# A two-layer decoder trunk on one core: joins that go behind the weight splits they held up, a table made later, an output in halves, and wo's row pairs in another order

## The chip, the cores and the metric

The kernel runs on one core of a Trainium2 chip. The metric is the device time of one execution in microseconds (us); less is better. The engines are named as in the profile: PE (TensorE, matmuls), DVE (VectorE), ACT (ScalarE), POOL (GpSimd) and SP (SyncE, which issues most DMAs here).

## The reference

A residual stream x of 256 tokens by 2048 columns passes through two layers. Layer 0 is retention with 8 heads and then an MLP; layer 1 is multi-head latent attention (MLA) with shared keys and values, and then an MLP. All is float32.

```python
for layer in range(DEPTH):
    if layer < N_A_LAYERS:
        x = x + retention(rms_norm(x, norm_mix[layer]), ret_w_in[layer], ret_w_out[layer], ...)
    else:
        # k_nope, k_pe, v from rms_norm(x, kv_norm_in) @ mla_w_kv_down, normed, @ mla_w_kv_up
        x = x + mla_attention(rms_norm(x, norm_mix[layer]), mla_w_dq[j], ..., mla_w_o[j], k_nope, k_pe, v, ...)
    x = x + jnp.square(jax.nn.relu(rms_norm(x, norm_mlp[layer]) @ mlp_w1[layer])) @ mlp_w2[layer]
```

Retention ends in `o * rsqrt(mean(o * o) + eps)`, times `silu(gate)`, times the output weights. Rotary tables (cos and sin of position times frequency) are made for retention and, with 64 columns, for MLA.

## The kernel before, in words

**Products.** Every weight is read once from memory as float32 into a `raw` buffer (three of them), by a DMA on SP's queue. ACT casts it to a high half `wh` (L206), DVE subtracts that from the weight for the low half `wl` (L207); this subtraction is called a low part here. Activations are split in the same way, and each product is three matmuls: high by high (L392), high by low (L393), low by high (L394). Five `wh` and five `wl` buffers go round.

**Row pairs.** Most products go through `gemm_pair`, which calls `quad` (L311) once for each of eight chunks of 256 weight rows (a row pair) by 1024 columns. A plain row pair is eight products of two-by-two blocks, 24 matmuls, and two low parts of 1024 columns. A seven is done by a scheme with seven products, 21 matmuls, for which DVE also forms sums of the weight blocks (L346, L355, L356) and then makes four low parts, one of 512 columns and three of 1024. Sevens have four extra accumulators, p1, p5, p6 and p7, which must be joined to the result after the last seven. `kinds` says which row pairs are sevens and `order` in which order they come. Row pair names in the rows have the number last: d_315 is row pair 5 of the second half of the last group of `w2`.

**The joins.** At the end of each MLP the second half of `w2` ends with plain row pairs behind the last seven, so `sums_into_x` (L159) joins the extra accumulators to x early: ACT copies p1 and p5, DVE forms v and u (L166, L167) and then adds or subtracts them in six instructions on x[.][2] and x[.][3] (L169, L171); p5 goes to both x[.][3]. When the last row pair is done, `rest_into_x` (layer 0) or `outside` (layer 1) adds the remaining accumulators (L517, L1167). In layer 0 the row pairs come in the order 0, 2, 4, 6, 1, 3, 5, 7 with sevens 1 and 3, in layer 1 in the order 0, 2, 1, 4, 3, 5, 6, 7 with sevens 1, 3 and 5. Behind layer 0 comes MLA's product with the kv-down weights (kd, by `piece`, L269 to L271), behind that dqp; behind layer 1 only the output.

**The order of the work.** The program is written out in Python, piece by piece (a piece is a chunk of weights). `later(n, fn)` puts a function in a list, to be called n pieces on; `tick` advances the clock and calls what is due. Each engine has its own queue of instructions, which it works off in order; a scheduler decides the order within each, and `queued_behind(ins, before)` makes one instruction stand behind another on the same engine. `low_part[0]` is always the low part made last. When an instruction at the head of a queue waits, all behind it wait as well.

**The tables.** `sincos` (L539) computes a table's angles on POOL by some 25 instructions. That for MLA, named `tm_`, is queued 12 pieces after the start of the first product; `mla_tables` (L589) makes sixteen small DVE instructions from it (`petab`, L598 and L601), 20 pieces after. For every head and each half of the tokens POOL also computes o_m and o_r, the inverse root of retention's norm, in `rstd` (L184, L186), from a sum that ACT makes (L201); DVE then makes y from it (L737), and PE transposes y into `ytp` (L225).

**wo.** MLA's output weights go through `gemm_blocks` (L460): two blocks of columns by `piece`, and then a pair of blocks, `wop`, by `gemm_pair`, in which row pairs 3, 5, 6 and 7 (`FOUR`) are sevens.

Of the kernel before, what the change touches and what calls it, by code (L numbers as in the profile page):

```python
# [16 lines left out]
ALU = mybir.AluOpType  # L17
# [18 lines left out]
P = 128  # L36
NT = 2
S = NT * P
# [9 lines left out]
QUERY, FOUR = (3, 4, 6, 7), (3, 5, 6, 7)  # L48
# [4 lines left out]
C_INVR, C_INVM, C_MASK, C_ID, C_ALL = 0, 128, 160, 544, 672  # L53
# [13 lines left out]
def yoco(ctx: ExitStack, tc: tile.TileContext, a):  # L67
    nc = tc.nc
# [25 lines left out]
    queue, low_part, first_low = [], [None], [None]  # L94
    clock, count, ahead = [0], itertools.count(), [None, None]

    def later(n, fn):
        queue.append((clock[0] + n, next(count), fn))
# [56 lines left out]
    def into_x(done, c, p, step=2):  # L155
        for j in range(2):
            later(step * j, lambda j=j: done(2 * p + j, [c[t][j] for t in range(NT)]))

    def sums_into_x(c, name):  # L159

        o = {}
        for key in ("p1", "p5"):
            o[key] = f2k([512], f"{name}_{key}")
            nc.scalar.copy(o[key], c[key])
        v, u = (f2k([512], f"{name}_{i}") for i in "vu")
        nc.vector.tensor_tensor(v, c["p6"], o["p1"], op=ALU.add)  # L166
        nc.vector.tensor_tensor(u, c["p7"], v, op=ALU.add)  # L167
        for t, j, part in ((0, 2, o["p1"]), (1, 2, u), (0, 3, o["p5"]), (1, 3, o["p5"])):
            nc.vector.tensor_tensor(x[t][j], x[t][j], part, op=ALU.add)  # L169
        for t, part in ((0, v), (1, u)):  # L170
            nc.vector.tensor_tensor(x[t][3], x[t][3], part, op=ALU.subtract)  # L171

    def rest_into_x(done, c):
        for j, keys in ((2, ("c11", "c21")), (3, ("c12", "c22"))):
            done(j, [c[key] for key in keys])

    def gain(col):
        return gains[:, col : col + 1]
# [126 lines left out]
    def queued_behind(ins, before):  # L305
        tc.add_manual_dep(
            ins.ins, before.ins.name,
            mybir.DependencyInfo(mybir.DependencyClass.NoSync, mybir.DependencyReason.DATA), reason="order",
        )
# [59 lines left out]
    def gemm_pair(w, chunk0, act, kinds, name, done, order=None, inner=None):  # L369

        made = {}
        total, count = {}, {}
        for seven in kinds:
            for key in ("c11", "c12", "c21"):
                total[key] = total.get(key, 0) + (1 if seven else 2)
            for key in ("p1", "p5", "p6", "p7") if seven else ("c22", "c22"):
                total[key] = total.get(key, 0) + 1

        def get(key):
            if key not in made:  # L380
                if key in ("p6", "p7"):
                    both = two_banks(f"{name}_p67")
                    made["p6"], made["p7"] = both[:, 0], both[:, 1]
                else:
                    made[key] = bank("tp" if key[0] == "p" else "acc", [512], f"{name}_{key}")
            return made[key]

        def mm(key, lhs, rhs):
            dst, n = get(key), count.get(key, 0)
            count[key] = n + 1  # L390
            (ah, al), (bh, bl) = lhs, rhs
            nc.tensor.matmul(dst, ah, bh, start=n == 0, stop=False)  # L392
            nc.tensor.matmul(dst, ah, bl, start=False, stop=False)  # L393
            nc.tensor.matmul(dst, al, bh, start=False, stop=n == total[key] - 1)  # L394

        order = order or range(len(kinds))
        sevens = [n for n, i in enumerate(order) if kinds[i]]
        for n, i in enumerate(order):
            need(act, i + 1)
            while kinds[i] and act[i][1] is None:  # L400
                run_first()
            v, more = act[i]
            quad(w, chunk0 + i, (v, more if kinds[i] else None), mm, f"{name}{i}")
            if inner is not None and n == sevens[-1]:
                queue.append((clock[0] + 1, -1, lambda: inner(made, name)))
            if n == len(kinds) - 1:
                queue.append((clock[0] + 1, -1, lambda: done(made) if inner else pair_out(made, name, done)))
            tick()
# [51 lines left out]
    def gemm_blocks(w, chunk_of, w_pair, act, nk, name, done):  # L460

        n = nk // 4
        parts = Firsts(act)
        first = [accs(512, f"{name}{b}") for b in range(2)]
        for g in range(n - 1):
            for b in range(2):
                need(act, 2 * g + 2)
                piece(w, chunk_of(b) + g, first[b], parts, g, nk, 512, f"{name}{b}")
        for b in range(2):
            need(act, 2 * n)  # L470
            last_piece(w, chunk_of(b), first[b], parts, nk, 512, f"{name}{b}", lambda acc, b=b: done(b, acc))
        gemm_pair(w_pair, 0, act, [k in FOUR for k in range(8)], f"{name}p", lambda c: into_x(done, c, 1))

    def x_block_t(blocks, b, g0s, outs, name, sums):

# [38 lines left out]
    def add_to_x(acc, b, ss, name):  # L514
        for t in range(NT):
            for part in acc[t] if isinstance(acc[t], tuple) else (acc[t],):
                nc.vector.tensor_tensor(x[t][b], part, x[t][b], op=ALU.add)  # L517
            if ss is not None:
                square_sum(x[t][b], ss[1][t][:, b : b + 1], f"{name}_{t}{b}")

# [18 lines left out]
    def sincos(inv, w, name):  # L539

        n = NT * w

        def f2k(shape, name):
            return shaped(act_tile(name, F32).rearrange("p j i s -> p (j i s)"), shape)

        ang = f2k([NT, w], f"{name}_ang")
        for t in range(NT):
            nc.gpsimd.tensor_scalar(ang[:, t], inv, pos_f[:, t : t + 1], None, op0=ALU.mult)
        flat = ang.rearrange("p t w -> p (t w)")
        k = f2k([2, n], f"{name}_k")  # L550
        for i in range(2):
            nc.gpsimd.tensor_scalar(k[:, i], flat, 1 / (2 * PI), 0.25 * i, op0=ALU.mult, op1=ALU.add)
        nc.gpsimd.tensor_scalar(k, k, MAGIC, -MAGIC, op0=ALU.add, op1=ALU.add)
        kh = f2k([2, n], f"{name}_kh")
        nc.gpsimd.tensor_scalar(kh, k, MAGIC_HI, -MAGIC_HI, op0=ALU.add, op1=ALU.add)
        kl = f2k([2, n], f"{name}_kl")
        nc.gpsimd.tensor_tensor(kl, k, kh, op=ALU.subtract)
        r = f2k([2, n], f"{name}_rr")
        both = flat.unsqueeze(1).to_broadcast([P, 2, n])
        part = f2k([2, n], f"{name}_part")  # L560

        def less(dst, src, kk, c):
            nc.gpsimd.tensor_scalar(part, kk, c, None, op0=ALU.mult)
            nc.gpsimd.tensor_tensor(dst, src, part, op=ALU.subtract)

        less(r, both, kh, c1)
        for kk, c in ((kl, c1), (kh, c2), (kl, c2), (k, c3)):
            less(r, r, kk, c)
        nc.gpsimd.tensor_scalar(r[:, 1], r[:, 1], PI / 2, None, op0=ALU.add)
        nc.gpsimd.tensor_scalar(k, r, 1 / (2 * PI), MAGIC, op0=ALU.mult, op1=ALU.add)  # L570
        nc.gpsimd.tensor_scalar(k, k, -MAGIC, None, op0=ALU.add)
        for c in (c1, c2 + c3):
# [84 lines left out]
    def start(half):  # L657
        first_inputs(half)
        if half == 3:
            nc.sync.dma_start(pos_i, a["pos"])  # L660
            nc.sync.dma_start(cst, a["cst"])
            nc.sync.dma_start(gpe, a["gpe"])
        if half == 5:
            ret_tables()
        if half == 7:
            for b in range(NB):
                later(2 + b, lambda b=b: load_x(b))
            later(6, scale_tables)
            later(12, lambda: mla_sc.append(sincos(cst[:, C_INVM : C_INVM + 32], 32, "tm")))
            later(20, mla_tables)  # L670

    def ret_rope(acc, out, name, wait):

# [483 lines left out]
    def leave(t, b):  # L1157
        nc.sync.dma_start(a["out"][t * P : (t + 1) * P, b * 512 : (b + 1) * 512], x[t][b])
# [4 lines left out]
            leave(t, b)  # L1163

    def outside(c):
        for t, j, key in ((0, 2, "c11"), (1, 2, "c21"), (0, 3, "c12"), (1, 3, "c22")):
            nc.vector.tensor_tensor(x[t][j], c[key], x[t][j], op=ALU.add)  # L1167
            leave(t, j)

    mlp(1, act, r, finish)  # L1170
    while queue:
# [94 lines left out]
```

## Time and profile before

| what | value |
|---|---|
| median of 3 runs | 2466.27 us (2465.57 to 2467.79) |
| profiled execution, its own time | 2468.5 us |
| its span in the trace | 2466.7 us |
| mean granted clock of PE | 0.998 |
| DMA, mean over the span | 211 GB/s |
| last PE matmul starts | 2461.30 us |

In timelines a row has the start, the length in us, the engine, the line and operation, output and inputs, and how many equal instructions in a run it stands for; in brackets the idle time of the engine before it and what ended that. Instructions overlap a little with their successors, so the distance between two starts, not the length, is what one costs in a full queue. In the table of waits a row has the total, the number of times and the longest.

### The profile page before, as it was taken

The numbers are of one execution on the slowest core, as the hardware profiler recorded it, in microseconds if no ns is written. First come the engines' busy times: TensorE is split into PE (matmuls) and PEld (weight loads), VectorE is DVE, ScalarE is ACT, GpSimd is POOL, SyncE is SP. The second block draws the span as 40 slices with busy tenths as digits, with TensorE's granted clock in tenths as the row PEclk, the third lists the DMA queues.
The fourth block names the chain that finished last, engine by engine and source line by source line (L and its number), as shares of the span: only waits on it lengthen the run. The fifth ranks groups of instructions, "written<-read, shape, count | busy, mean of one in ns | idle before, by whom it ended". The sixth has DMA issues, their size and how long they took to land.

```text
span 2466.7 us, 31692 instructions
## 1 busy us (share of the span) xinstructions
PE 2447.1 (99%) x11605; PEld 2060.3 (84%) x11605; DVE 2210.9 (90%) x2917; ACT 1641.3 (67%) x2306; POOL 237.7 (10%) x287
## 2 busy tenths in 40 slices
PE   9999999999999999999999999999999999999998
PEld 7888888888888888888888788998888888888887
DVE  7799899889899999999999998777899999999998
ACT  6566666556677767667676677577677667676674
POOL 6300001000000010010110001101000100100100
PEclk9999999999999999999999999999999999999999
DMA  8555569556565596695786555444555876957864
GB/s 310 197 196 201 177 200 265 198 174 223 204 212 199 193 264 208 209 268 188 239 257 216 184 205 179 154 163 171 187 207 204 252 226 197 264 200 221 263 219 154
DMA packets 93404, 521.05 MB, mean 211 GB/s; under 512 B 11072, under 2 KB 12224, under 8 KB 40000
## 3 DMA queue, kind: packets, MB, share of 16 engines
q1 hardware_dynamic: 71856, 472.83, 55.7%
q0 software_dynamic: 21248, 46.15, 8.8%
q8 instruction: 91, 1.49, 0.2%
q14 instruction: 65, 0.53, 0.1%
q10 hardware_dynamic: 144, 0.05, 0.0%
HBM read 479.14 MB, written 39.85 MB: 210 GB/s over the span
## 4 chain that ended last, share of the span: by engine, by line
PE 97%; DVE 2%; ACT 0%; issue 0%; POOL 0%; DMA 0%; SPq 0%; ACTq 0%; DVEq 0%
PE u_c L394 7%; PE u_c L392 7%; PE u_c L393 7%; PE d_c L393 7%; PE d_c L394 7%; PE d_c L392 7%; PE rp_c L394 3%; PE rp_c L393 3%; PE rp_c L392 3%; PE rq_acc L297 2%; PE rk_acc L297 2%; PE u_p L394 2%; PE u_p L393 2%; PE u_p L392 2%; PE d_p L393 2%; PE d_p L394 2%
## 5 line engine op out<-in xcount | busy, mean ns | idle before, releaser
L207 DVE TENSOR_TENSOR u_wl<-u_raw,u_wh 128x1024 fp32r<-128x1024 f32 (+1 forms) x256 | 278.7, 1109 | 30.9 <-ACT u_wh L206 30.9
L207 DVE TENSOR_TENSOR d_wl<-d_raw,d_wh 128x1024 fp32r<-128x1024 f32 (+1 forms) x256 | 277.8, 1107 | 29.0 <-ACT d_wh L206 28.9
L393 PE MATMUL d_c<-d_wl,hid 128*128 128x512 f32 x706 | 275.8, 391 | 4.8 <-DVE d_wl L207 4.8
L392 PE MATMUL u_c<-u_wh,n 128*128 128x512 f32 x712 | 277.4, 391 | 0.0
L394 PE MATMUL u_c<-u_wh,n 128*128 128x512 f32 x712 | 277.2, 389 | 0.0
L393 PE MATMUL u_c<-u_wl,n 128*128 128x512 f32 x712 | 277.2, 389 | 0.0
L394 PE MATMUL d_c<-d_wh,hid 128*128 128x512 f32 x706 | 275.8, 391 | 0.0
L392 PE MATMUL d_c<-d_wh,hid 128*128 128x512 f32 x706 | 274.6, 392 | 0.5 <-ACT d_wh L206 0.5
L206 ACT CAST u_wh<-u_raw 128x1024 fp32r<-128x1024 f32 (+1 forms) x256 | 241.1, 973 | 48.0 <-PE u_c L394 21.2
L206 ACT CAST d_wh<-d_raw 128x1024 fp32r<-128x1024 f32 (+1 forms) x256 | 240.2, 972 | 42.8 <-ACT d_wh L206 16.0
L206 ACT CAST d_wh<-d_u 128x1024 fp32r<-128x1024 f32 x106 | 107.7, 1051 | 118.5 <-DVE d_u L356 65.4
L206 ACT CAST u_wh<-u_u 128x1024 fp32r<-128x1024 f32 x104 | 106.3, 1052 | 115.8 <-DVE u_u L356 59.5
L393 PEld LDWEIGHTS d_c<-d_wl,hid 128*128 128x128 f32 x706 | 133.0, 188 | 33.2 <-DVE d_wl L207 6.1
L394 PEld LDWEIGHTS u_c<-u_wh,n 128*128 128x128 f32 x712 | 133.7, 188 | 27.8
L206 ACT CAST rp_wh<-rp_raw 128x1024 fp32r<-128x1024 f32 x112 | 104.0, 945 | 79.3 <-PE rp_c L394 53.7
L392 PEld LDWEIGHTS d_c<-d_wh,hid 128*128 128x128 f32 x706 | 132.9, 188 | 28.4 <-ACT d_wh L206 1.4
L393 PEld LDWEIGHTS u_c<-u_wl,n 128*128 128x128 f32 x712 | 133.7, 188 | 27.3
L392 PEld LDWEIGHTS u_c<-u_wh,n 128*128 128x128 f32 x712 | 133.7, 188 | 27.1
L394 PEld LDWEIGHTS d_c<-d_wh,hid 128*128 128x128 f32 x706 | 133.0, 188 | 27.7
L207 DVE TENSOR_TENSOR rp_wl<-rp_raw,rp_wh 128x1024 fp32r<-128x1024 f32 x112 | 119.3, 1085 | 18.0 <-ACT rp_wh L206 17.9
L207 DVE TENSOR_TENSOR d_wl<-d_u,d_wh 128x1024 fp32r<-128x1024 f32 x106 | 125.5, 1217 | 0.0
L207 DVE TENSOR_TENSOR u_wl<-u_u,u_wh 128x1024 fp32r<-128x1024 f32 x104 | 123.1, 1217 | 2.0 <-ACT u_wh L206 1.6
(568 smaller groups left out, 6501.3 us busy)
## 6 DMA issues: line engine op xcount, KB each, us to landing
u_raw<-in_mlp_w SPq DMA_DIRECT2D x128, 1024.0 KB, 5.5
d_raw<-in_mlp_w SPq DMA_DIRECT2D x128, 1024.0 KB, 4.9
rp_raw<-in_ret_w_gv SPq DMA_DIRECT2D x56, 1024.0 KB, 4.9
ro_raw<-in_ret_w_out SPq DMA_DIRECT2D x32, 1024.0 KB, 5.0
uq_raw<-in_mla_w_uq SPq DMA_DIRECT2D x24, 768.0 KB, 4.3
rq_raw<-in_ret_w_qk SPq DMA_DIRECT2D x16, 1024.0 KB, 4.9
rk_raw<-in_ret_w_qk SPq DMA_DIRECT2D x16, 1024.0 KB, 4.9
xh<-d_c POOLq DMA_DIRECT2D x48, 256.0 KB, 6.1
```

The costliest lines, as they stand in the source:

```text
L206: nc.scalar.copy(h, src)
L207: return nc.vector.tensor_tensor(l, src, h.bitcast(F32), op=ALU.subtract)
L297: nc.tensor.matmul(acc[f], wh[:, cols], a.rearrange("p i s -> p (i s)"), start=k == 0, stop=k == nk - 1)
L392: nc.tensor.matmul(dst, ah, bh, start=n == 0, stop=False)
L393: nc.tensor.matmul(dst, ah, bl, start=False, stop=False)
L394: nc.tensor.matmul(dst, al, bh, start=False, stop=n == total[key] - 1)
```

## The change

1. `sums_into_x` is called two pieces instead of one after the last seven; its v and its additions are queued behind the low part made last by then, and the four instructions on x[.][3] come a piece later still (`join_rest`). In `rest_into_x` the additions for the second block of columns come half a piece after those for the first, and in `add_to_x` those of x[.][2] and x[.][3] at the end of layer 0 (`n2`) are queued behind the low part made last.
2. MLA's table is made 18 instead of 12 pieces after the start, and `mla_tables` comes at 26 instead of 20.
3. In `outside` the last block x[1][3] is added and written in two halves of 256 columns, one DMA on ACT's queue and one on SP's.
4. The pair of blocks of wo takes its row pairs in the order 0, 1, 2, 3, 5, 4, 6, 7.

```diff
-        nc.vector.tensor_tensor(v, c["p6"], o["p1"], op=ALU.add)
+        queued_behind(nc.vector.tensor_tensor(v, c["p6"], o["p1"], op=ALU.add), low_part[0])
         nc.vector.tensor_tensor(u, c["p7"], v, op=ALU.add)
-        for t, j, part in ((0, 2, o["p1"]), (1, 2, u), (0, 3, o["p5"]), (1, 3, o["p5"])):
-            nc.vector.tensor_tensor(x[t][j], x[t][j], part, op=ALU.add)
-        for t, part in ((0, v), (1, u)):
-            nc.vector.tensor_tensor(x[t][3], x[t][3], part, op=ALU.subtract)
+
+        def join(*parts):
+            for t, j, part, op in parts:
+                queued_behind(nc.vector.tensor_tensor(x[t][j], x[t][j], part, op=op), low_part[0])
+
+        join((0, 2, o["p1"], ALU.add), (1, 2, u, ALU.add))
+        join_rest = (0, 3, o["p5"], ALU.add), (1, 3, o["p5"], ALU.add), (0, 3, v, ALU.subtract), (1, 3, u, ALU.subtract)
+        queue.append((clock[0] + 1, -1, lambda: join(*join_rest)))
 
     def rest_into_x(done, c):
         for j, keys in ((2, ("c11", "c21")), (3, ("c12", "c22"))):
-            done(j, [c[key] for key in keys])
+            later(j / 2 - 0.5, lambda j=j, keys=keys: done(j, [c[key] for key in keys]))
...
-                queue.append((clock[0] + 1, -1, lambda: inner(made, name)))
+                queue.append((clock[0] + 2, -1, lambda: inner(made, name)))
...
+            lambda c: into_x(done, c, 1), order=(0, 1, 2, 3, 5, 4, 6, 7),
...
-                nc.vector.tensor_tensor(x[t][b], part, x[t][b], op=ALU.add)
+                added = nc.vector.tensor_tensor(x[t][b], part, x[t][b], op=ALU.add)
+                if name == "n2" and b >= 2:
+                    queued_behind(added, low_part[0])
...
-            later(12, lambda: mla_sc.append(sincos(cst[:, C_INVM : C_INVM + 32], 32, "tm")))
-            later(20, mla_tables)
+            later(18, lambda: mla_sc.append(sincos(cst[:, C_INVM : C_INVM + 32], 32, "tm")))
+            later(26, mla_tables)
...
-        for t, j, key in ((0, 2, "c11"), (1, 2, "c21"), (0, 3, "c12"), (1, 3, "c22")):
+        for t, j, key in ((0, 2, "c11"), (1, 2, "c21"), (0, 3, "c12")):
             nc.vector.tensor_tensor(x[t][j], c[key], x[t][j], op=ALU.add)
             leave(t, j)
+        for i, queue_ in enumerate((nc.scalar, nc.sync)):
+            part = slice(i * S, (i + 1) * S)
+            nc.vector.tensor_tensor(x[1][3][:, part], c["c22"][:, part], x[1][3][:, part], op=ALU.add)
+            queue_.dma_start(a["out"][P:, 3 * 512 + i * S : 3 * 512 + (i + 1) * S], x[1][3][:, part])
```

POOL's queue around the first head's o_m and o_r (so_931 and so_940 are the sums of the two token halves; `tm_` is MLA's table), before:

```order
L184 TENSOR_SCALAR o_m<-so_931 128x1
L186 TENSOR_TENSOR o_r<-o_m,neg_half 128x1
L548 TENSOR_SCALAR tm_ang<-cst,pos_f 128x32 x2
L552 TENSOR_SCALAR tm_k<-tm_ang 128x64 x2
L553 TENSOR_SCALAR tm_k<-tm_k 128x128
L555 TENSOR_SCALAR tm_kh<-tm_k 128x128
L557 TENSOR_TENSOR tm_kl<-tm_k,tm_kh 128x128
L563 TENSOR_SCALAR tm_part<-tm_kh 128x128
L564 TENSOR_TENSOR tm_rr<-tm_ang,tm_part 128x128
L184 TENSOR_SCALAR o_m<-so_940 128x1
L186 TENSOR_TENSOR o_r<-o_m,neg_half 128x1
```

and now (the lines lie four, later nine, further down in the changed file):

```order
L188 TENSOR_SCALAR o_m<-so_931 128x1
L190 TENSOR_TENSOR o_r<-o_m,neg_half 128x1
L188 TENSOR_SCALAR o_m<-so_940 128x1
L190 TENSOR_TENSOR o_r<-o_m,neg_half 128x1
L557 TENSOR_SCALAR tm_ang<-cst,pos_f 128x32 x2
```

The ten table instructions that stood between the two halves' pairs now stand behind both. On DVE the sixteen `petab` instructions stand together, ahead of the low parts of head 2's later weights, instead of in groups among those of head 1's.

DVE's queue at the end of layer 0's MLP, before (d_313 and d_315 are row pairs 3 and 5, d_317 the last; d_31_p the extra accumulators and their copies, x_mlp_12009 and x_mlp_12090 blocks of x):

```order
L207 TENSOR_TENSOR d_313_wl_12499<-d_313_u_12466,d_313_wh_12498 128x1024
L169 TENSOR_TENSOR x_mlp_12009<-x_mlp_12009,d_31_p_12508 128x512
L207 TENSOR_TENSOR d_315_wl_12525<-d_315_raw,d_315_wh_12524 128x1024
L166 TENSOR_TENSOR d_31_v<-d_31_p_12442,d_31_p_12508 128x512
L169 TENSOR_TENSOR x_mlp_12090<-x_mlp_12090,d_31_p_12510 128x512
L167 TENSOR_TENSOR d_31_u<-d_31_p_12442,d_31_v 128x512
L169 TENSOR_TENSOR x_mlp_12090<-x_mlp_12090,d_31_p_12510 128x512
L169 TENSOR_TENSOR x_mlp_12009<-x_mlp_12009,d_31_u 128x512
L171 TENSOR_TENSOR x_mlp_12090<-x_mlp_12090,d_31_v 128x512
L171 TENSOR_TENSOR x_mlp_12090<-x_mlp_12090,d_31_u 128x512
L207 TENSOR_TENSOR d_315_wl_12541<-d_315_raw,d_315_wh_12540 128x1024
L207 TENSOR_TENSOR d_317_wl_12559<-d_317_raw,d_317_wh_12558 128x1024
```

and now:

```order
L211 TENSOR_TENSOR d_315_wl_12511<-d_315_raw,d_315_wh_12510 128x1024
L211 TENSOR_TENSOR d_315_wl_12527<-d_315_raw,d_315_wh_12526 128x1024
L166 TENSOR_TENSOR d_31_v<-d_31_p_12442,d_31_p_12542 128x512
L171 TENSOR_TENSOR x_mlp_12009<-x_mlp_12009,d_31_p_12542 128x512
L167 TENSOR_TENSOR d_31_u<-d_31_p_12442,d_31_v 128x512
L211 TENSOR_TENSOR d_317_wl_12555<-d_317_raw,d_317_wh_12554 128x1024
L171 TENSOR_TENSOR x_mlp_12009<-x_mlp_12009,d_31_u 128x512
L211 TENSOR_TENSOR d_317_wl_12571<-d_317_raw,d_317_wh_12570 128x1024
L171 TENSOR_TENSOR x_mlp_12090<-x_mlp_12090,d_31_p_12544 128x512 x2
L171 TENSOR_TENSOR x_mlp_12090<-x_mlp_12090,d_31_v 128x512
L171 TENSOR_TENSOR x_mlp_12090<-x_mlp_12090,d_31_u 128x512
L211 TENSOR_TENSOR kd_wl_12598<-kd_raw,kd_wh_12597 128x640
```

Both low parts of row pair 5 stand ahead of all joins, those of row pair 7 ahead of five of them; two of the four last additions (L524) follow behind each of the next two kd low parts. Layer 1's end is changed in the same way, with row pairs 6 and 7 (d_316, d_317) in the places of 5 and 7.

DVE's queue at the end of wo's pair of blocks, before, from the last low part of row pair 3 on (wop_u are the sums of a seven; the second row is row pair 4's):

```order
L207 TENSOR_TENSOR wop_wl_16403<-wop_u_16368,wop_wh_16402 128x1024
L207 TENSOR_TENSOR wop_wl_16416<-wop_raw,wop_wh_16415 128x1024
L346 TENSOR_TENSOR wop_u_16449<-wop_raw 128x1024
L207 TENSOR_TENSOR wop_wl_16432<-wop_raw,wop_wh_16431 128x1024
L355 TENSOR_TENSOR wop_u_16450<-wop_u_16449,wop_raw 128x512
L356 TENSOR_TENSOR wop_u_16450<-wop_u_16450,wop_raw 128x512
```

and now:

```order
L350 TENSOR_TENSOR wop_u_16415<-wop_raw 128x1024
L211 TENSOR_TENSOR wop_wl_16403<-wop_u_16368,wop_wh_16402 128x1024
L359 TENSOR_TENSOR wop_u_16416<-wop_u_16415,wop_raw 128x512
L360 TENSOR_TENSOR wop_u_16416<-wop_u_16416,wop_raw 128x512
L211 TENSOR_TENSOR wop_wl_16421<-wop_raw,wop_wh_16420 128x1024
L211 TENSOR_TENSOR wop_wl_16431<-wop_raw,wop_wh_16430 128x512
```

The sums and low parts of row pair 5 follow row pair 3's at once; the two low parts of the plain row pair 4 stand behind them, and then come 6 and 7.

More of the change, by code (lines that the diff above doesn't have):

```diff
@@ L471, in gemm_blocks @@
             last_piece(w, chunk_of(b), first[b], parts, nk, 512, f"{name}{b}", lambda acc, b=b: done(b, acc))
-        gemm_pair(w_pair, 0, act, [k in FOUR for k in range(8)], f"{name}p", lambda c: into_x(done, c, 1))
+        gemm_pair(
+            w_pair, 0, act, [k in FOUR for k in range(8)], f"{name}p",
+            lambda c: into_x(done, c, 1), order=(0, 1, 2, 3, 5, 4, 6, 7),
+        )
     def x_block_t(blocks, b, g0s, outs, name, sums):
```

## The prediction

> **What bounds the kernel now.** I read the busy line first, then the chain that ended last, then the table of what PE waited for, and then the timelines around each of those waits.
>
> ```profile
> PE 2447.1 (99%) x11605; PEld 2060.3 (84%) x11605; DVE 2210.9 (90%) x2917; ACT 1641.3 (67%) x2306; POOL 237.7 (10%) x287
> PE 97%; DVE 2%; ACT 0%; issue 0%; POOL 0%; DMA 0%; SPq 0%; ACTq 0%; DVEq 0%
> ```
>
> PE is the bound: it makes 97% of the chain, and no matmul is added or removed by the change. So all that can be won is time in which PE stands still or runs slowly, and the next table says for whom it stood still (total, times, longest).
>
> ```profile
> PE rg_acc L269 <- ACT a L208: 5.2, 1, 5.2
> PE d_c L393 <- DVE d_wl L207: 4.8, 3, 2.3
> PE ytp L225 <- DVE y L737: 2.4, 1, 2.4
> PE wop_c L392 <- ACT wop_wh L206: 0.4, 1, 0.4
> ```
>
> The first is the start of the kernel, which the diff doesn't touch. The other three rows, 7.6 us together, are the places at which the diff's edits aim. The clock that PE was granted adds to two of them (start, length, then busy time of PE, PEld, DVE, ACT and POOL with counts, granted clock, DMA):
>
> ```profile
> 105.64:109.06 3.42, 3.42 (x10) 2.64 (x9) 3.42 (x6) 0.02 (x1) 3.00 (x6) 0.50 0.14 55
> 1402.70:1406.10 3.40, 3.40 (x10) 2.66 (x9) 2.49 (x3) 0.53 (x1) 0.00 (x0) 0.50 0.77 253
> 2454.10:2457.50 3.40, 3.37 (x15) 2.79 (x16) 2.25 (x2) 0.00 (x0) 0.00 (x0) 1.00 0.00 0
> ```
>
> After the wait for y and after the longest wait in layer 0 the clock was 0.50 for 3.4 us; after the shorter one in layer 1 it stayed at 1.00. What a half clock costs is seen in matmul starts:
>
> ```profile
> 1402.54 0.46 PE L393 MATMUL d_c<-d_wl,hid 128*128 128x512 f32 x1
> 1406.18 0.39 PE L394 MATMUL d_c<-d_wh,hid 128*128 128x512 f32 x1
> 2451.14 1.07 PE L392 MATMUL d_c<-d_wh,hid 128*128 128x512 f32 x4
> ```
>
> At full clock four such matmuls take 1.07 us from the first start to the last end and one takes 0.39 (last two rows), so they start (1.07 - 0.39) / 3 = 0.227 us apart, the pitch. Nine starts lie from 1402.54 up to 1406.18: 3.64 us instead of 9 x 0.227 = 2.04. So one half-clock stretch costs 1.6 us.
>
> **Part 1, the later rotary table.** For the first head, y of the second token half needs o_r from POOL.
>
> ```profile
> 100.48 0.19 ACT L201 ACTIVATION_READ_ACCUMULATOR o_sq<-o 128x1 f32 x1
> ```
> ```profile
> 97.28 0.90 POOL L548 TENSOR_SCALAR tm_ang<-cst,pos_f 128x32 f32<-128x32 f32 x2
> 103.11 0.19 POOL L184 TENSOR_SCALAR o_m<-so 128x1 f32<-128x1 f32 x1
> 103.39 0.57 POOL L186 TENSOR_TENSOR o_r<-o_m,neg_half 128x1 f32<-128x1 f32 x1
> ```
> ```profile
> 104.00 0.75 DVE L737 SCALAR_TENSOR_TENSOR y<-o,o_r,gate 128x512 f32<-128x512 f32 x1 [2.47 <-POOL o_r L186]
> ```
> ```profile
> 102.02 0.40 PE L392 MATMUL rp_c<-rp_wh,a 128*128 128x512 f32 x1
> 104.80 0.66 PE L225 MATMUL ytp<-cst,y 128*128 128x128 f32 x4 [2.38 <-DVE y L737]
> ```
>
> The sum was ready at 100.67 (0.19 after 100.48), but POOL took it up only at 103.11, since the table's instructions stood ahead of it. With the table later, o_m starts near 100.7 and o_r ends 0.85 us after that, at 101.6. DVE has been free since 104.00 - 2.47 = 101.53, so y starts at 101.6 and the transposes 0.80 after it (104.80 - 104.00), at 102.4. That takes 2.4 us off the wait, and about 0.15 stays (the last matmul's successor could start at 102.25). With a wait of 0.15 the half clock behind it goes too: **-2.4 - 1.6 = -4.0**. What is late next is DVE, in the stretch behind:
>
> ```profile
> 116.30:163.00 46.70, 46.70 (x225) 39.07 (x224) 46.61 (x72) 32.33 (x44) 0.09 (x1) 1.00 0.56 191
> 146.20 0.18 DVE L598 SCALAR_TENSOR_TENSOR petab<-tm_sc,gpe 128x32 f32<-128x32 f32 x1
> 146.30 0.18 DVE L601 SCALAR_TENSOR_TENSOR petab<-tm_sc,gpe 128x32 f32<-128x32 f32 x1
> ```
>
> DVE is busy for 46.61 of these 46.70 us, so PE, 4.0 earlier, must be followed by a DVE that is only 2.4 earlier. But the sixteen small table instructions, 0.10 apart, leave this stretch with the change (the order puts them behind all rows of it): 16 x 0.10 = 1.6 us. The two amounts balance, so I count nothing here and keep 1.6 as what it costs if they don't. The table itself is needed only in MLA, whose first product starts at 1410.53 (below); POOL is busy 10%.
>
> **Part 2a, layer 0's joins.** DVE at the end of the first MLP, then PE:
>
> ```profile
> 1394.29 0.68 DVE L169 TENSOR_TENSOR x_mlp<-x_mlp,d_p 128x512 f32<-128x512 f32 x1
> 1394.89 1.22 DVE L207 TENSOR_TENSOR d_wl<-d_raw,d_wh 128x1024 fp32r<-128x1024 f32 x1
> 1396.03 0.68 DVE L166 TENSOR_TENSOR d_v<-d_p,d_p 128x512 f32<-128x512 f32 x1
> 1400.24 3.49 DVE L207 TENSOR_TENSOR d_wl<-d_raw,d_wh 128x1024 fp32r<-128x1024 f32 x3
> ```
> ```profile
> 1395.23 0.40 PE L394 MATMUL d_p<-d_wh,hid_more 128*128 128x512 f32 x1
> 1396.16 0.50 PE L393 MATMUL d_c<-d_wl,hid 128*128 128x512 f32 x1 [0.54 <-DVE d_wl L207]
> 1398.12 1.07 PE L392 MATMUL d_c<-d_wh,hid 128*128 128x512 f32 x4
> 1401.51 0.50 PE L393 MATMUL d_c<-d_wl,hid 128*128 128x512 f32 x1 [2.32 <-DVE d_wl L207]
> ```
>
> Eight joins, 0.60 apart, stand before the second low part of row pair 5 (one ahead of the first low part, seven from 1396.03 to 1400.24). By the order shown above they now stand behind both. (The pitch of DVE is read here too: 1396.03 - 1394.89 = 1.14 for 1024 columns, and 1400.24 - 1396.03 over seven joins = 0.60 for 512.) The first low part starts at 1394.29 instead of 1394.89: the matmul of 1396.16 comes 0.60 earlier. The second follows at once and ends near 1396.6, while PE asks for it at 1398.4: of the wait from the last of four starts, 1398.80, to 1401.51, all but one pitch goes, 2.71 - 0.23 = 2.48. The matmul after a wait takes 0.11 longer than the pitch, and the half clock goes as well: -0.60 - 2.48 - 0.11 - 1.6 = **-4.8**. Row pair 7's low parts come at 1399.6 and 1401.3 (three joins of 0.60, a low part of 1.14, a join, a low part), PE wants them about 1400.5 and 1403.
>
> What is late next is the kv-down product (kd). d_c ends near 1405.6 instead of 1410.5, but five of the joins and the four additions of the last accumulators, 0.60 each, now stand among kd's low parts.
>
> ```profile
> 1405.60:1450.00 44.40, 44.40 (x284) 40.81 (x284) 35.81 (x75) 34.08 (x75) 4.68 (x7) 0.99 0.65 218
> 1405.57 0.73 ACT L206 CAST kd_wh<-kd_raw 128x640 fp32r<-128x640 f32 x1 [6.47 <-DMA kd_raw<-in_mla_w_kv_down]
> 1410.53 0.30 PE L269 MATMUL kd_acc<-kd_wh,n 128*128 128x320 f32 x1
> ```
>
> DVE has 44.4 - 35.8 = 8.6 us free there; PE has none. Placing the rows one behind another I find kd's first low part at 1404.5 (wanted 1405.6), its second at 1406.5 (wanted 1407.3), the third at 1408.5 (wanted 1409.1). The second kd load, which ended at 1405.57 since its buffer was held by the late low part, starts 4.8 earlier. Every slack is under 1.1 us where it was several; a miss of 0.1 to 0.2 at three or four of them is likely: **+0.4**, between 0 and, if the nine 0.60s that moved in are half uncovered, 2.7.
>
> **Part 2b, layer 1's joins.** The same, with output behind it instead of kd.
>
> ```profile
> 2452.86 3.48 DVE L207 TENSOR_TENSOR d_wl<-d_raw,d_wh 128x1024 fp32r<-128x1024 f32 x3
> ```
> ```profile
> 2454.13 0.50 PE L393 MATMUL d_c<-d_wl,hid 128*128 128x512 f32 x1 [1.92 <-DVE d_wl L207]
> ```
>
> The last of the four starts from 2451.14 on is 2451.82; 2454.13 - 2451.82 - 0.23 = 2.08, and 0.11 behind it. The second low part of row pair 6 starts without the eight joins at 2452.86 - 8 x 0.60 = 2448.06 and ends at 2449.2; three joins, a low part, a join and a low part behind it, row pair 7's end at 2452.2 and 2453.9, and PE wants them at 2452.0, 2454.0 and 2456.7: **-2.2**. The clock had not dropped here, so nothing more.
>
> **Part 3, wo's order.** Row pairs 5, 6 and 7 of the seven-product kind came in a row; DVE gives each one 6.4 us (sums of 1024, 512 and 512 columns, low parts of 512 and three times 1024, at the 1.14 and 0.60 of the rows of part 2a) against 21 x 0.227 = 4.8 of PE, and so falls behind.
>
> ```profile
> 1776.55 0.39 PE L392 MATMUL wop_c<-wop_wh,ot 128*128 128x512 f32 x1
> 1777.36 0.50 PE L392 MATMUL wop_c<-wop_wh,ot 128*128 128x512 f32 x1 [0.42 <-ACT wop_wh L206]
> ```
>
> Now there are two and two with a plain one between, and the x_wo addition stands behind the last. The gap, 0.81 - 0.23 = 0.58, with its 0.11, goes: **-0.7**.
>
> **Part 4, output in halves.**
>
> ```profile
> 2460.40 2.37 SPq L1158 DMA_DIRECT2D out<-x_mlp  x4
> DMA to landing us min/median/max: 2.5/3.0/6.6
> gains<-in_gains ACTq DMA_DIRECT2D x1, 49.0 KB, 3.3
> ```
>
> The second row is that of the output's eight DMAs of 256 KB. 49 KB on ACT's queue took 3.3: by these rows a smaller transfer isn't a shorter one. An output of 128 KB is not in the trace; the bounds are -0.5 (the quickest of the eight against their median) and +0.4 (the 0.3 that ACT's DMA took beyond that median, and 0.1, an estimate, for one instruction more). I take 0, since the row of the smaller DMA lies nearest: **0**.
> The Trainium skill, "DMA: Bandwidth & Descriptors", section "Anatomy of one DMA — SWDGE (gpsimd) path", gives a fixed part of about 2.0 us and a part that grows with the bytes at 436 GB/s. By it, as an estimate, halving 256 KB saves 0.3 us; the 49 KB row speaks against that.
>
> **Sum:** -4.0 - 4.8 + 0.4 - 2.2 - 0.7 + 0 = -11.3 on the profiled execution's 2468.5, that is 2457.2. The three timed runs lie at 2465.57 to 2467.79, 0.7 to 2.9 below that execution; their spread of 2.2 is more than one half-clock stretch. If the median loses all 11.3, it comes to 2455.0; if the median's run lacked one of the two stretches, to 2456.6. I forecast **2456.0**.
>
> **Rivals.**
> *The clock drops belong to this execution.* For: the waits of 2.5 us dropped the clock and the one of 2.1 did not, so a timed run may have had neither. Then only waits are won, 11.3 - 3.2 = 8.1, and 2466.27 - 8.1 = 2458.2. Against: the profiled time agrees with the slowest run to 0.7. Chance 0.12.
> The Trainium skill, "TensorE: Matmul & The Clock Gate", section "Part 1: The HAM clock gate (the "warmup" mystery)", has a free-running window of 3413 ns and a drop after at least one idle window. The 3.4 us stretches agree with that length; drops after waits of 2.5 us don't agree with a wholly idle window.
> *The cover fails.* DVE cannot follow in 116 to 163 (1.6 comes back), and kd pays its 2.7 instead of 0.4: -11.3 + 3.9 = -7.4, 2458.9. For: DVE full, slacks under 1.1. Against: the sixteen instructions that leave. Chance 0.13.
> *Slower.* In kd and the dqp product behind it, the queued-behind additions wait for PE's last accumulators, a low part waits behind them, its raw buffer is freed late, and the next load costs a full 4 us exposed, which delays PE and so the next turn. It decides once a low part comes over 4 us late; with five such turns, 5 x 4.0 = 20 us lost against 11.3 won: 2475. For: the 6.47 us that ACT waited for kd_raw. Against: that buffer is freed 4.8 earlier now. Chance 0.04.
> *It doesn't do what it says*, or most is lost by a cause unseen: the order shows the rows moved, so only 0.06, near 2464.
>
> **How the numbers follow.** The forecast has 0.65, the rivals 0.12, 0.13, 0.04 and 0.06. 0.2% is 4.9 us, about what a measurement of this kernel can tell from no change: faster means below 2461.3. Forecast and first two rivals lie there: 0.90; same 0.06, slower 0.04. Range 2453.0 (halves gain 0.5, no loss in kd, median as the profile, and 1 for the runs' spread) to 2460.5 (cover fails, plus half of the runs' spread of 2.2 and the half's 0.4).
>
> **What would show it.** The rows y, d_c and wop_c gone from PE's waits; clock 1.00 behind them; POOL's o_m near 100.7; d_c ending near 1405; no new wait at kd over 0.5. It is wrong if PE waits for rp_wl or rq_wl before 163, or for kd_wl, n or dqp_wl behind 1405.

## The result and the profile after

| | before | changed |
|---|---|---|
| median of 11 runs | 2467.77 us (2465.57 to 2468.72) | 2460.99 us (2459.74 to 2461.83) |
| profiled execution, own time | 2468.5 us | 2459.74 us |
| span in the trace | 2466.7 us | 2457.9 us |
| ratio | | 0.9973, 95% interval 0.9964 to 0.9983 |

The change makes the kernel 6.8 us faster. The forecast was 2456.0, and its range ended at 2460.5, half a microsecond below the time. The three runs of the kernel before that were known then had a median of 2466.27; eight more raised it to 2467.77. So the gain was 6.8 where 10.3 had been forecast. The pair of profiled executions differs by more than the medians, 8.8 us.

The changed kernel's page, busy line, and then what PE waited for (total, times, longest):

```profile
PE 2443.7 (99%) x11605; PEld 2057.9 (84%) x11605; DVE 2212.0 (90%) x2918; ACT 1641.5 (67%) x2306; POOL 238.7 (10%) x287
```
```profile
PE rg_acc L273 <- ACT a L212: 5.4, 1, 5.4
PE sc L717 <- DVE y L211: 0.6, 1, 0.6
PE ytp L229 <- DVE y L746: 0.5, 1, 0.5
...
PE kd_acc L275 <- DVE n L213: 0.3, 1, 0.3
PE rp_c L396 <- DVE rk_u L686: 0.3, 1, 0.3
...
PE kpe_tp L229 <- DVE kpp L958: 0.2, 1, 0.2
...
PE n_tp L229 <- ACT n2u L496: 0.2, 1, 0.2
```

The 4.8 us for d_wl and the 0.4 for wop_wh are gone, and y is down from 2.4 to 0.5. In their place stand small waits which the kernel before didn't have: sc and rk_u behind the first place, n, n_tp and kpe_tp at kd.

The table of waits leaves out the slower matmul behind a wait and the clock. So I added up from the matmul starts of each trace by how much each distance between two starts exceeds the pitch for its width (0.227 us for 512 columns, 0.173 for 384, 0.147 for 320, 0.118 for 256, 0.109 for 128; shorter distances count against it). "H" marks a stretch with a half clock. The names of the experiments stand below.

| PE's excess in us, from ... to ... | before | e1 tables | e2 joins, layer 0 | e3 joins, layer 1 | changed | changed again | e10 |
|---|---|---|---|---|---|---|---|
| 101 to 200 (first head) | 5.8 H | 4.0 | 4.7 | 4.7 | 3.5 | 3.5 | 3.6 |
| 200 to 1385 (no edit's work) | 4.4 | 5.0 | 6.1 | 4.6 | 4.4 | 4.5 | 4.3 |
| 1385 to 1402 (end of layer 0) | 4.1 | 4.1 | 0.9 | 4.1 | 0.9 | 0.9 | 0.9 |
| 1402 to 1455 (kd, dqp) | 2.6 H | 1.0 | 2.6 | 0.9 | 2.5 | 2.3 | 1.4 |
| 1455 to 2400 (with wo) | 5.5 | 5.6 | 6.7 | 5.5 | 4.9 | 4.8 | 4.8 |
| 2400 to the end | 3.3 | 3.3 | 3.3 | 1.0 | 1.1 | 1.1 | 1.0 |

This table is where the 8.8 us of the two profiled executions come from: 2.3 + 3.2 + 0.1 + 0.6 + 2.2 = 8.4, and 0.4 at the start of the kernel, of which the output takes 0.2 back. The row from 200 to 1385 shows what one trace may differ from another without any edit, up to 1.7 us: most of it is one wait for n between 1375 and 1381, which is 0 in one trace and 1.3 in another. So a single trace's difference of some tenths proves little, and the rows that carry the argument are those that agree in all traces with the same edit, as the 0.9 and the 4.1 at the end of layer 0 do.

### The profile page after: what moved, and what is told of

It is laid out like the page before. It is cut to its first block, busy times and chain, and to the rows that moved or that the text cites. A ratio compares the mean times of both kernels' runs of the same rounds, so it can differ in the third digit from the quotient of the medians.

```text
span 2457.9 us, 31701 instructions
## 1 busy us (share of the span) xinstructions
PE 2443.7 (99%) x11605; PEld 2057.9 (84%) x11605; DVE 2212.0 (90%) x2918; ACT 1641.5 (67%) x2306; POOL 238.7 (10%) x287
## 4 chain that ended last, share of the span: by engine, by line
PE 90%; DVE 4%; issue 1%; ACT 1%; DMA 0%; POOL 0%; DVEq 0%; ACTq 0%
PE u_c L398 7%; PE u_c L397 7%; PE u_c L396 7%; PE d_c L398 7%; PE d_c L396 7%; PE d_c L397 7%; PE rp_c L396 2%; PE rp_c L398 2%; PE rp_c L397 2%; PE u_p L398 2%; PE u_p L397 2%; PE u_p L396 2%; PE ro_c L396 2%; PE ro_c L398 2%; PE ro_c L397 2%; PE d_p L396 2%
```

## The experiments

Theories: **W**, the parts are worth their waits and half clocks as the profile before shows them, less what DVE and kd take back. **C**, later made exact as **G**: the half clocks are not in every execution. **D**: what part 1 wins is given back, since DVE is full behind it. **K**: kd's loss comes from the place of layer 0's last additions.

### e1_tables: part 1 alone

```diff
-            later(12, lambda: mla_sc.append(sincos(cst[:, C_INVM : C_INVM + 32], 32, "tm")))
-            later(20, mla_tables)
+            later(18, lambda: mla_sc.append(sincos(cst[:, C_INVM : C_INVM + 32], 32, "tm")))
+            later(26, mla_tables)
```

> The kernel before with part 1 alone (tables 18 and 26 instead of 12 and 20). Theory W (the waits and half clocks of the profile are in every execution, and DVE, which follows only 2.3 us earlier, takes 1.2 of the gain back): PE's wait for y falls from 2.4 to about 0.5, the half clock behind it goes, waits of 0.7 near 113 and 0.5 near 172 appear; PE is 2.2 us earlier at 200, time -2.2 us. Theory C (the half clock belongs to the profiled execution only): the profile may show it, but timed runs gain only the waits, 1.8 - 1.2 = 0.6 us.

Measured: median 2466.97 against 2468.53, ratio 0.9992 (0.9984 to 1.0001), so by the medians about 1.6 us of the 4.0 that the sum had given it. In the trace the wait for y falls to 0.5, and the waits for sc (0.6) and for rk_u (0.8; 0.3 in the changed kernel) appear as in the changed kernel. The interval, -3.9 to +0.2 us, holds both theories and no change at all, so the time doesn't decide between them. The trace loses the half clock and 1.8 us of excess from 101 to 200.

### e2_joins0: part 2 in layer 0 alone, and e3_joins1: in layer 1 alone

In e2 the joins, `rest_into_x` and `add_to_x` are as in the change for layer 0, and the joins of layer 1 as before; e3 is the other way round, with `rest_into_x` and `add_to_x` as before.

```diff
-                queue.append((clock[0] + 1, -1, lambda: inner(made, name)))
+                queue.append((clock[0] + (1 if inner is sums_now else 2), -1, lambda: inner(made, name)))
```

> The kernel before with part 2 for layer 0 alone. Theory W: d_c ends 4.8 us earlier, kd and what follows give 1.4 back in waits for n, n_tp and kpe_tp; time -3.4 us. Theory C: no half clock in timed runs, -1.8 us. If the waits at kd come only from the combination with the tables, -4.8.

Measured: 2465.85 against 2468.53, ratio 0.9990 (0.9981 to 0.9998), -2.7 us. Of the excess at the end of layer 0, 3.2 goes, and at kd 1.6 is given back; that is there without the tables too, so it isn't a matter of the combination.

> The kernel before with part 2 for layer 1 alone. All theories: the wait of 1.9 for d_wl at the end goes, -2.2 us in the profile and in timed runs; no clock was lost there. If the time moves by less than 1, something behind the last matmul took it.

Measured: 2465.67, ratio 0.9990 (0.9982 to 0.9999), -2.9 us; the trace has 2.2 less at the end and nothing given back. This part is worth what the sum said. The sentence "no clock was lost there" is wrong, as e4's trace shows.

What e2 and e3 show besides is the clock. Both have part 1's wait of 2.4 us unchanged, e3 the long one of layer 0 too, and behind none of them the clock is down.

### e4_wo: part 3 alone

```diff
-        gemm_pair(w_pair, 0, act, [k in FOUR for k in range(8)], f"{name}p", lambda c: into_x(done, c, 1))
+        gemm_pair(
+            w_pair, 0, act, [k in FOUR for k in range(8)], f"{name}p",
+            lambda c: into_x(done, c, 1), order=(0, 1, 2, 3, 5, 4, 6, 7),
+        )
```

> The kernel before with part 3 alone. The wait of 0.4 for wop_wh goes, -0.7 us; with a spread of 2 us between runs the timed difference may not show it, so the profile is asked.

Measured: 2468.60 against 2468.53, ratio 0.9999 (0.9990 to 1.0008). The wait for wop_wh is gone from the trace; three others, for u_wl and hid_tp at 2293 to 2336, add 1.1 there that no other trace has at this place; e2 has two like them, 0.8 together, at 1975 and 2143. So 0.6 to 0.7 is shown by the traces, with the changed kernel's row above, and not by the time. In this trace the clock dropped behind the wait of layer 1 and not behind y.

### The clock: the windows of four traces

The clock drops for stretches of 3.413 us, and in each trace these lie on one grid of that length, which starts elsewhere in each execution: in the kernel before the two half clocks start at 105.65 and 1402.71, 380 lengths apart, in e4 at 1400.68 and 2455.40, 309 lengths apart. The windows view, cut on that grid (start and end, length, busy us of PE, PEld, DVE, ACT and POOL with counts, granted clock, DMA share, GB/s), first of the kernel before, each window with the one behind it (that behind 1402.71, at 0.50, stands in the prediction):

```profile
102.23:105.65 3.42, 1.04 (x8) 0.85 (x8) 1.62 (x4) 0.66 (x3) 2.91 (x7) 1.00 0.88 343
105.65:109.06 3.41, 3.41 (x10) 2.63 (x9) 3.41 (x6) 0.02 (x1) 2.98 (x6) 0.50 0.14 55
1399.30:1402.71 3.41, 1.20 (x5) 1.03 (x6) 3.41 (x5) 0.00 (x0) 0.00 (x0) 1.00 0.09 17
...
2450.61:2454.02 3.41, 1.60 (x8) 0.98 (x6) 3.41 (x6) 0.00 (x0) 0.00 (x0) 1.00 0.00 0
2454.02:2457.43 3.41, 3.30 (x14) 2.74 (x15) 2.33 (x3) 0.00 (x0) 0.00 (x0) 1.00 0.00 0
```

Then e4, at the ends of both layers:

```profile
1397.26:1400.68 3.42, 1.24 (x6) 0.69 (x4) 3.42 (x5) 0.73 (x1) 0.00 (x0) 1.00 0.00 0
1400.68:1404.09 3.41, 3.27 (x8) 2.60 (x9) 3.41 (x5) 0.00 (x0) 0.00 (x0) 0.50 0.61 198
2451.98:2455.40 3.42, 1.52 (x7) 0.96 (x6) 3.42 (x5) 0.00 (x0) 0.00 (x0) 1.00 0.00 0
2455.40:2458.81 3.41, 3.41 (x9) 2.64 (x8) 1.22 (x2) 0.00 (x0) 0.00 (x0) 0.50 0.00 0
```

And e3, whose wait for y and whose wait at the end of layer 0 are the kernel before's:

```profile
100.45:103.87 3.42, 2.84 (x16) 2.05 (x14) 1.92 (x2) 2.69 (x6) 3.10 (x5) 1.00 0.34 62
103.87:107.28 3.41, 1.60 (x10) 1.47 (x11) 2.37 (x5) 0.00 (x0) 2.90 (x7) 1.00 0.90 359
107.28:110.69 3.41, 3.41 (x16) 2.81 (x15) 3.38 (x6) 1.43 (x3) 2.98 (x6) 1.00 0.01 2
1397.52:1400.93 3.41, 1.57 (x7) 0.95 (x6) 3.41 (x6) 0.73 (x1) 0.00 (x0) 1.00 0.00 0
1400.93:1404.34 3.41, 2.91 (x13) 2.42 (x14) 3.41 (x5) 0.00 (x0) 0.00 (x0) 1.00 0.55 183
```

In all fourteen traces, windows in which PE was busy for 1.52 us or less are followed by a half clock, and those with 1.57 or more are not. A wait of 2.5 us that a grid line cuts left at least 1.57 busy on both sides of it and cost nothing more. The traces of before, e1, e2, e3, e4, e8 and e12 hold 17 waits for y and d_wl of about their old lengths, 2.1 to 2.7 us from start to start (e12's longer one for y left out); 5 were followed by a half clock.

### e8_longwait and e12_longwait2: a longer wait for y

e8 makes one instruction of the table on POOL twice; e12 puts a long one into it (e12's edit):

```diff
+        if name == "tm":
+            many = f2k([8, 2 * n], f"{name}_many")
+            nc.gpsimd.tensor_scalar(
+                many, k.rearrange("p i n -> p (i n)").unsqueeze(1).to_broadcast([P, 8, 2 * n]), 1.0, None, op0=ALU.mult
+            )
```

> The kernel before with one instruction of the table on POOL made twice, so that the wait for y is about 4.2 us instead of 2.5. Theory G (the clock is decided in fixed windows of 3.41 us, whose phase differs from run to run, and drops when about 0.60 of one window is idle; a wait of 2.5 does that in about half of the runs, one of 4.2 always): a half clock of 3.41 us behind y in the profile, the mean clock of no timed run above that of the kernel before with one drop, 0.999, time +1.6 to +2.4 us. Rival H (drops come at random or by temperature): some runs at 1.000, as the kernel before has.

e8 did not make the wait that it was built for: the scheduler put o_m one instruction earlier, the two took 2.35 us together instead of 1.63 for one, and PE's excess at y was 2.7 instead of 2.55. Cut by a grid line, it left no window with less than 2 us busy, and no half clock followed. Time 2468.28 against 2468.75, ratio 0.9999 (0.9990 to 1.0008). It tells nothing on longer waits.

> The kernel before with a long instruction (128x1024) put into the table on POOL, so that the wait for y is 3.5 us or more. Theory G (fixed windows, a half clock when about 0.60 of one is idle): a half clock behind y in the profile; more runs at a mean clock of 0.998 than the kernel before has; time +2 us. Rival H (drops at random): no half clock behind y in the profile, clocks spread as in the kernel before.

```profile
103.48:106.90 3.42, 0.85 (x7) 0.85 (x8) 1.62 (x4) 0.00 (x0) 2.94 (x8) 1.00 0.78 311
106.90:110.31 3.41, 3.41 (x10) 2.64 (x9) 3.41 (x6) 0.01 (x1) 3.15 (x4) 0.50 0.00 0
```

e12's wait is 3.5 us; a window with 0.85 busy, and the half clock behind it. Time 2470.32 against 2468.68, ratio 1.0006 (0.9997 to 1.0014). Of its 11 timed runs 2 had a mean clock of 0.997, 6 of 0.998 and 3 of 0.999. Of the kernel before, 66 runs in three jobs, 13 had 0.998, 50 had 0.999 and 3 had 1.000; of the changed kernel, 17 runs, 12 had 1.000 and 5 had 0.999. The rounded values are coarse, but they shift as theory G says, and chance drops would not follow the length of one wait. The time itself shows little: of the 1.6 us between the medians the longer wait makes 1.2, and the interval includes no change at all.

### e7_sum7 and e13_nosum: DVE's work behind y

e7 forms two of head 1's activation sums earlier; e13 leaves one of them out, and with it a part of the computation.

```diff
-            later({2: 10, 4: 14.6, 6: 18, 7: 19}[c] - clock[0], sum_up)
+            later({2: 10, 4: 13.6, 6: 14.6, 7: 19}[c] - clock[0], sum_up)
```
```diff
             def sum_up():
+                if c == 6:
+                    sums0[c] = sums0[4]
+                    return
```

> The changed kernel with two of the four activation sums of head 1 formed about a piece and three pieces and a half earlier, so that about 2 us of DVE's work stand ahead of the stretch from 102 to 116 instead of in it. Theory D (DVE, full in that stretch and only 2.3 us earlier, makes the waits for sc at 113 and for rk_u at 172): the wait of 0.7 at sc goes, PE is 0.7 to 1.0 earlier behind it; time -0.7. Rival: the wait at sc stays, since it is the transposes' bank of PSUM that comes free late by PE's own order.

e7 was a miss: 2462.59 against 2468.75, ratio 0.9975 (0.9964 to 0.9986), no better than the changed kernel. sc came earlier in PE's order and waited 0.6 at 107, and waits of 0.5 and 0.4 for rp_wl at 125 and 141 came instead; the excess from 101 to 200 was 4.7. Moving DVE's work in a stretch that DVE fills moved the wait.

> The changed kernel without the activation sums of chunk 6: row pair 6 of the seven-product kind uses chunk 4's, so that part of the computation is left out. About 2 us less of DVE between 102 and 130. Theory D (DVE is full in that stretch and makes PE wait): PE's excess between 101 and 200 us falls from 3.5 to 2.5 or less, time -1 us or more against the changed kernel. Rival (PSUM banks and PE's own order make the waits): excess and time stay.

e13's excess from 101 to 200 is 2.8, 0.7 less, and the waits at 113 and 172 are gone; one of 0.5 for sc at 105 is new. This doesn't support theory D: the new wait makes up for that at 113, and that at 172 is also missing in e9, which has no edit there. Nor does the time show a gain (2461.08 against 2460.93 for the changed kernel in the same job). In its trace kd lost 1.6 more, by a longer load (below).

### e6_rest_now, e10_rest_half and e9_best: layer 0's last additions, and the output

e6 puts `rest_into_x` and `add_to_x` back; e10 only makes the additions half a piece earlier; e9 is e10 with `outside` as it was before.

```diff
-            later(j / 2 - 0.5, lambda j=j, keys=keys: done(j, [c[key] for key in keys]))
+            later(j / 2 - 1, lambda j=j, keys=keys: done(j, [c[key] for key in keys]))
```

> The changed kernel with the last additions of layer 0 as they were: both columns' additions at once behind the last row pair, none of them queued behind a low part. Theory K (kd's 1.4 us come from the additions that stand half a piece later, so that the transposes of n come a kd half later and have too little cover): the waits for n and n_tp at kd fall from 0.8 to under 0.3, time 0.5 to 1 us below the changed kernel. Rival J (they come from d_c ending 4.8 earlier, whatever the additions' place): waits of about 1 us stay, or a wait for kd_wl of 1 us or more appears, time as the changed kernel's or above.

> The changed kernel with the last additions of layer 0 half a piece earlier (0 and 0.5 instead of 0.5 and 1.0 pieces behind the last row pair), still queued behind low parts. Theory K: waits for n and n_tp at kd gone, 0.5 to 0.8 us below the changed kernel. Rival J: the same sum of waits at kd.

e6: 2459.64 against 2468.75, ratio 0.9966 (0.9953 to 0.9978), excess at kd 1.7. e10: 2459.78, ratio 0.9964 (0.9951 to 0.9976), excess at kd 1.4. The changed kernel has 2.3 and 2.5, the kernels without part 2a 0.9 and 1.0. e2, e7 and e13, which have the additions in the changed kernel's place, have 2.6, 3.2 and 3.9. So the place of the additions makes about 1.0 of the 1.5; a rest of 0.4 stays (e10 waits for kd_wl, 0.2, and n_tp). The mechanism is seen in the changed kernel's ACT and PE:

```profile
1408.85 1.35 ACT L210 CAST kd_wh<-kd_raw 128x640 fp32r<-128x640 f32 x2 [2.34 <-PE n_tp L229]
1410.11 0.47 ACT L212 ACTIVATE n<-n_tp,gains 128x256 fp32r<-128x256 f32 x1
```
```profile
1402.91 0.30 PE L273 MATMUL kd_acc<-kd_wh,n 128*128 128x320 f32 x1
1408.19 1.04 PE L229 MATMUL n_tp<-cst,x_mlp 128*128 128x128 f32 x8
1411.62 0.42 PE L275 MATMUL kd_acc<-kd_wh,n 128*128 128x320 f32 x1 [0.34 <-DVE n L213]
```

and in e10:

```profile
1406.47 0.47 ACT L212 ACTIVATE n<-n_tp,gains 128x256 fp32r<-128x256 f32 x1
```

The eight transposes of n stand 36 matmuls (5.3 us) behind the first of kd, 24 (3.5 us) in the kernel before. ACT must turn them into n, but its queue has two kd casts ahead, which stood still for 2.34 us. The row puts this wait down to PE, whose signal happened to come 0.04 us after the load's. In the other four traces with the additions at this place (changed again, e2, e7, e13) the same row names the load, as in the changed kernel again:

```profile
1408.74 1.36 ACT L210 CAST kd_wh<-kd_raw 128x640 fp32r<-128x640 f32 x2 [2.18 <-DMA kd_raw<-in_mla_w_kv_down]
```

The chain of work that ended last between 1400 and 1412 goes through the load in the changed kernel's first trace too (start, length, what):

```profile
1402.83 0.82 DVE kd_wl L211
1403.66 0.02 issue
1403.67 5.09 DMA kd_raw<-in_mla_w_kv_down
...
1408.85 0.74 ACT kd_wh L210
```

The fourth kd load could be issued only when the second low part, which stands behind two of the additions, had freed its raw buffer; it landed at 1408.77, and the cast started 0.08 later. In all five traces the cast starts 0.08 behind that landing, and kd's excess grows with the load's length as much as the load does: 4.97 us and 2.3 (changed again), 5.09 and 2.5 (changed), 5.24 and 2.6 (e2), 5.89 and 3.2 (e7), 6.56 and 3.9 (e13). In the kernel before, one cast stands ahead of n, and its load had landed 3 us earlier. With the additions half a piece earlier ACT takes n at 1406.47, ahead of the cast that waits for the fourth load, though that load is no earlier.

> The changed kernel once more, as the measure for the other three. Time 2460.0 to 2461.5; in its trace no window of 3.41 us with 0.60 of PE's time idle, and no half clock between 12 and 2450 us.

The changed kernel once more: 2460.93 against 2468.68, ratio 0.9970 (0.9958 to 0.9982), -7.75 us; its trace repeats the first one to 0.2 in each stretch, with no half clock between 12 and 2450.

> The changed kernel with the last additions of layer 0 half a piece earlier and the last output block whole again. Theory K: kd's excess 1.0 us below the changed kernel's 2.5. For the output: from the last matmul's start to the span's end 5.35 to 5.45 us as in the kernel before, against 5.6 in halves. Time 1.0 to 1.3 us below the changed kernel of the same job. Rival: the halves were worth something, and the time stays.

e9: 2458.86 in the same job, ratio to the kernel before 0.9963 (0.9950 to 0.9975), the fastest median of all. Its interval overlaps the changed kernel's, so the time alone doesn't prove it better; its trace has 0.9 less at kd than the changed kernel's of that job, and 0.9 more at the wait for n at 1376, which no edit touches. From the last matmul's start to the end of the span it takes 5.37 us. With whole output blocks eight traces have 5.35 to 5.39; in halves four have 5.59 to 5.61 and two 5.26 and 5.31. So the halves won nothing, and lost 0.2 in most.

## Why the prediction was wrong, point by point

**What bounds it, and which waits go.** Right. PE is the bound, and the excess at the end of layer 0, at wo and at the end of layer 1 fell by 3.2, 0.6 and 2.2; the sum had 3.2, 0.7 and 2.2.

**The half clocks: the first step that failed.** "With a wait of 0.15 the half clock behind it goes too" and "the half clock goes as well" count two half clocks in the kernel before, and the forecast lies between losing both and losing one in the median's run. They depend on how the 3.41 us grid falls on a wait. The mean clocks of the timed runs, 0.99885 for the kernel before and 0.99971 for the changed one, differ by 0.00086; one stretch makes 0.5 x 3.41 / 2466 = 0.0007. That is about 1.2 stretches or 2.0 us, and 5 of 17 waits make 0.9 of three, or 1.4 us. The sum had 3.2; both figures are estimates, and slightly high, since behind y a half clock costs less (below). The rival "the clock drops belong to this execution", at 0.12, was nearer to what happens than the forecast. Part 2b's "the clock had not dropped here, so nothing more" failed in the same way, to the other side.

**Part 1: the second.** "The two amounts balance, so I count nothing here" failed. The sixteen small instructions leave DVE only from 133 us on, but the first new wait is at 113, before any of them:

```profile
113.62 1.27 DVE L211 TENSOR_TENSOR y<-ytp,y 128x512 fp32r<-128x512 f32 x2
```
```profile
114.44 0.45 PE L717 MATMUL sc<-rq_q,rk_q 128*128 128x256 f32 x1 [0.57 <-DVE y L211]
```
```profile
102.00:116.00 14.00, 12.90 (x61) 10.65 (x62) 13.90 (x21) 6.67 (x11) 12.59 (x19) 1.00 0.44 172
```

From 102 to 116 DVE is busy 13.90 of 14.00 us. The longer PE is held at y, the less it loses at sc: 0.7 at y and 0.7 to 0.8 at sc in the changed kernel and e1, 2.6 and 0.6 in e2, e3 and e4, 2.7 and 0.2 in e8, and 0.1 at sc with a half clock behind y (before, e12). This speaks for DVE and against PE's own order, the rival that e7's expectation names. The traces of e2 and e3, which have the old wait without the half clock, show that the price was partly there before: with PE 1.6 earlier they wait 0.6 at sc as well. So a half clock behind y costs 1.1 and not 1.6 there, and from 4.7 in those two the excess falls to 3.5: part 1 brings 1.2 where the sum had 2.4 for the wait and 1.6 for the clock. Of the 2.4, 0.2 is lost at sc and 0.5 at 172, and 0.5 more at y, where 0.7 and not 0.15 stays:

```profile
100.32 0.72 POOL L188 TENSOR_SCALAR o_m<-so 128x1 f32<-128x1 f32 x1 [3.47 <-ACT o_sq L205]
101.13 0.56 POOL L190 TENSOR_TENSOR o_r<-o_m,neg_half 128x1 f32<-128x1 f32 x1
```
```profile
100.31 0.69 DVE L211 TENSOR_TENSOR a0s_more<-a0s_sum,a0s_more 128x512 fp32r<-128x512 f32 x1
```

o_m starts right behind its sum, as forecast, but takes 0.72 instead of 0.19; it ends 0.05 us behind the DVE instruction that ran beside it, as every o_m with such a neighbour does (last section).

**Part 2a's kd: the third, a path that the working left out.** It put +0.4 where 1.5 came, within its bounds of 0 to 2.7. "Every slack is under 1.1 us" was said of the low parts, and PE waited for none of them in kd. What came late was n: the working placed the low parts on DVE, but not the loads that each of them lets start, nor ACT's queue, where n stood behind casts that needed the fourth load. The rival "Slower" names this path, a raw buffer freed late and the next load exposed, with five turns of 4 us; here it was one turn. A wait for n behind 1405 is also one of the prediction's own signs of being wrong, and it came.

**Part 4** was 0 and came to +0.2, inside its bounds.

**The sum again:** -1.2 - 3.2 + 1.5 - 0.6 - 2.2 + 0.2 = -5.5 for the waits, and 1.4 to 2.0 for half clocks make -6.9 to -7.5. The two jobs measured -6.8 and -7.75. The rest of the error in the absolute time is the median that the sum was laid on, 2466.27 of three runs, 1.5 below that of eleven.

The Trainium skill, "TensorE: Matmul & The Clock Gate", section "Part 1: The HAM clock gate (the "warmup" mystery)", has a free-running window of 3413 ns, and the grid of the traces agrees. It lets the clock fall after at least one idle window; here a window with 1.52 us of PE busy was enough, 45% of it, and the measurement decides.

**Settled and open.** That the clock is decided by such windows is shown by the traces; how many half clocks a median run has is only estimated, from rounded means. That kd's loss comes from the fourth load ahead of n in ACT's queue is shown by the five traces and by e10. That DVE makes the wait for sc rests on the rows, DVE full and PE waiting for its y, and on how the loss there shrinks when PE comes later; neither e7 nor e13, which took work from DVE in that stretch, won it back, so what would is open. Why two traces with halves end in 5.3 us is open.

## What to carry to other kernels

Before a slow stretch of the clock goes into a sum, see whether it is in every execution: one profile shows one fall of the grid, and a wait of 2.5 us was followed by a half clock in some executions and not in others. A wait that is taken away moves PE ahead of every engine that was just keeping up: a gain of 4 us on PE needs as much on the engine beside it, and from the very next place, not on average over the stretch. When work is delayed, follow what it feeds through all queues, also through the load that can start only when the delayed work has freed its buffer, and the queue whose head waits for that load. Where a row puts a wait down to an engine, see whether a load landed just before.

## What the runs showed of the hardware that was not expected

- The clock's grid has a sharp edge here: PE busy 1.52 us of a window of 3.41 was followed by half clock, 1.57 was not.
- How long a POOL instruction on one column (o_m) took went with DVE. Of the 224 o_m rows in the fourteen traces, 98 had no DVE instruction beside them and took 0.19 us; the other 126 took up to 1.29 and ended 0.05 to 0.06 us behind the DVE instruction that ran beside them. No experiment changed that DVE instruction alone.
- An output in two halves on two queues ended no earlier than one whole block: 5.26 to 5.61 us behind the last matmul's start, against 5.35 to 5.39.
